# A fused RWKV-7, attention and MLP layer: the second tile of tokens is transposed as it comes, and its norm applied behind the products

## The chip, the cores and the metric

The kernel is one program on one core of a Trainium2 chip. The time is the device time of one execution in microseconds (us). The core has a matrix engine (TensorE, PE in the profile; its weight loads are listed apart as PEld), three engines for elementwise work (VectorE or DVE, ScalarE or ACT, GpSimd or POOL) and a queue for DMAs (SyncE, SP). Each engine works through its own list of instructions in order; semaphores make one engine wait for another.

## The reference, cut to what matters

One decoder layer on 256 tokens of 1024 numbers. The input is normalised, and one wide projection feeds three users:

```python
h = rms_norm(x, norm1_g[l])          # x * rsqrt(mean(x*x) + 1e-6) * g, per token
proj = h @ w_in[l]                   # (256, 1024) @ (1024, 5408)
z_rwkv, z_moba, gate_pre = ...       # columns 0:1824, 1824:3360, 3360:5408
z_rwkv = z_rwkv + rwkv_mu[l] * (shift_right(z_rwkv) - z_rwkv)   # mix with the token before
y_a = rwkv7_time_mix(z_rwkv, ...)    # r, k, v (512 columns each), xw, xa, xg (low rank)
q = partial_rope(rms_norm(q, q_norm_g[l]), positions)           # and k alike
y_b = moba_attention(q, k, v)        # here: causal attention over 256 tokens
x = x + (sigmoid(gate_a) * (y_a @ w_branch_a) + sigmoid(gate_b) * (y_b @ w_branch_b)) @ w_out
x = x + conv_ffn(rms_norm(x, norm2_g[l]), ...)
```

A norm's number per token (1 / root of the mean square) is a factor of a whole row of `h`, so it may as well be applied to the row of a product `x*g @ w`.

## The kernel before

**Precision.** Every wide product is made of three passes: a float32 operand is split into a rounded high part and the rest, and high*high, high*low and low*high are summed. For each 512 KB block of weights (`raw`, 128x1024), ScalarE makes the high part (`whi`, line L263) and VectorE the low part (`wlo`, L273); there are 122 such blocks, 4 raw, 4 high and 3 low buffers. A raw buffer is loaded again when its low part is done. The activations' parts are `hh` and `hl` (one tile `hx`).

**Staging.** `first_steps` is written out by hand for all engines: the load of x (two tiles of 128 tokens, four DMAs of 256 KB), the squares and root of each tile (`ss`, `rs`), the scaled rows `xn`, eight transposes per tile into PSUM (`xt`, L427), the split into `hh` and `hl` (L434, L436, L439) and the first products with the blocks 0 and 1 (`first`, L466, the columns of xw, xa, xg). Matrix-engine dummies (`keep_warm`, L388) run ahead of and between the transposes. Then two threads run, interleaved by hand-given costs: `bulk` makes the projections in order (k, r, q, v, attention's v, a gate, attention's k, seven gates, the branches), and `chain` the RWKV recurrence. TensorE's order comes from that interleaving, and the orders of VectorE, ScalarE and GpSimd from a scheduler that places instructions by estimated times.

**What the steps below touch.** `proj2` makes 256 columns of a projection over all tokens in one PSUM tile `p` (two groups of 128 columns by 256 tokens) from two blocks. `shift(dst, p, i)` turns it into a mixed `z`: one ScalarE instruction (L364) that reads `p`, then one of VectorE (L365). `finish_qk` norms attention's q and k per head; `rotate` applies the rotary angles on VectorE (L1061 to L1064). `group_norm` norms the recurrence's output, one chunk of 64 tokens at a time; GpSimd makes the power -1/2 (L931) and VectorE multiplies (L932).

Of the kernel before, what the change touches and what calls it, by code (L numbers as in the profile page):

```python
# [19 lines left out]
D = 1024  # L20
# [16 lines left out]
def body(tc, x, positions, norm1_g, w_in, rwkv_mu, w_decay_up, decay_bias, w_aaa_up,  # L37
# [5 lines left out]
    with ctx:  # L43
# [22 lines left out]
        def b2(name, shape, dt=F32):  # L66
            return sb.tile(shape, dt, name=name, tag="b2", bufs=9)
# [71 lines left out]
        G1, MU, DB, AB, KK_, KA, RK, LG, LB = 0, 8, 23, 27, 31, 35, 39, 43, 47  # L139
        omm = cst.tile([128, 15], F32, name="omm")  # L140
        omka = cst.tile([128, 4], F32, name="omka")

        pts = []

# [14 lines left out]
        def col(i):  # L159
            return par[:, i:i + 1]  # L160

        wdu = cst.tile([128, CW], F32, name="wdu")
# [197 lines left out]

        mixed = []

        def shift(dst, p, i):
            act.activation(dst, p, AF.Copy, scale=omm[:, i:i + 1])  # L364
            mixed.append(dve.scalar_tensor_tensor(dst[:, 1:S], p[:, 0:S - 1], col(MU + i), dst[:, 1:S],  # L365
                                                  op0=OP.mult, op1=OP.add).ins)
# [3 lines left out]
        def first_steps():  # L370
# [15 lines left out]
            def keep_warm(n):  # L386
                for _ in range(n):
                    pe.matmul(p, ones[:, 0:128], ones, start=True, stop=True)  # L388
# [10 lines left out]
            rs = sb.tile([128, 2], F32, name="rs1")  # L399
            bk = [b("xt") for b in (chp, chp, chp, atp, atp, acc, acc)]  # L400

            def at(k):
                return bk[min(k, 6)][:, 0 if k < 7 else 256:256 if k < 7 else 512]

            for t in range(2):
                xn = [b2("xn1", [128, 512]) for _ in range(2)]
                for hf in range(2):
                    act.activation(xn[hf], x_sb[t][:, hf * 512:hf * 512 + 512], AF.Square,
                                   accum_out=ss[:, t, hf:hf + 1])
                    if hf == 0:  # L410
                        dve.tensor_scalar(ss[:, t, 0:1], ss[:, t, 0:1], 1.0 / D, NORM_EPS,
                                          op0=OP.mult, op1=OP.add)
                act.activation(rs[:, t:t + 1], ss[:, t, 1:2], AF.Sqrt, scale=1.0 / D, bias=ss[:, t, 0:1])
                dve.reciprocal(rs[:, t:t + 1], rs[:, t:t + 1])
                for hf in range(2):
                    src = x_sb[t][:, hf * 512:hf * 512 + 512]
                    if t and hf:
                        act.activation(xn[hf], src, AF.Copy, scale=rs[:, t:t + 1])
                    else:
                        dve.tensor_scalar(xn[hf], src, rs[:, t:t + 1], None, op0=OP.mult)  # L420
                if t == 0:
                    pt = bk[5][:, 256:264]
                    pe.transpose(pt, p0, ident[:8, :8])
                    keep_warm(2)
                    dve.tensor_copy(par[:, 0:8], pt)
                for k in (0, 1, 2, 3, 4, 6, 7, 5):
                    pe.transpose(at(k)[:, t * 128:t * 128 + 128], xn[k // 4][:, k % 4 * 128:k % 4 * 128 + 128],  # L427
                                 ident)
                if t == 0:
                    keep_warm(3)  # L430

            def high(k):
                if k in (1, 3):
# [9 lines left out]
            for b in range(2):  # L443
# [4 lines left out]
            raw, hi, lo = w[0]  # L448
            for cs in (slice(0, 512), slice(512, 1024)):
                pool.tensor_copy(hi[:, cs], raw[:, cs])  # L450
            for k in range(8):
                high(k)
            for cs in (slice(0, 512), slice(512, 1024)):
                pool.tensor_tensor(lo[:, cs], raw[:, cs], hi[:, cs].bitcast(F32), op=OP.subtract)
            act.copy(w[1][1], w[1][0])
            for k in range(8):
                low(k)
            raw, hi, lo = w[1]
            for cs in (slice(0, 512), slice(512, 1024)):
                pool.tensor_tensor(lo[:, cs], raw[:, cs], hi[:, cs].bitcast(F32), op=OP.subtract)  # L460

            def first(b, lo_, xx, ks=(0, 1, 2, 3)):
                wv = w[b][lo_ + 1].rearrange("p (k c) -> p k c", k=4)
# [4 lines left out]
                                  skip_group_check=True)  # L468

            pts.append(atp("pt"))  # L470
            first(0, 0, hh)
            first(0, 1, hh, (0, 1))
            first(0, 0, hl)
            first(0, 1, hh, (2, 3))
            params_turned()
            late_params()
            split_hi()
# [2 lines left out]
            split_lo()  # L480

            first(1, 0, hh)
            first(1, 1, hh, (0, 1))
            first(1, 0, hl)
            first(1, 1, hh, (2, 3))
            late_consts()
            tl = chp("tl")[:, 0:S]
            for n, xx in enumerate((hh, hl)):
# [9 lines left out]
            dve.tensor_copy(tls, tl)  # L498
            shift(xg, p[:, 256:512], 13)
            split_lo()  # L500
            split_hi()
# [7 lines left out]
        def proj2():  # L509
            p = acc()  # L510
            yield from wst(p, 2, hh, hl)
            return p

        def now(gen):
# [48 lines left out]
        def chain():  # L563
# [352 lines left out]
            def group_norm():  # L916

                for c in range(4):
                    yield from need(c, ny)
                    y = ny[c]  # L920
                    cs = slice(64 * c, 64 * c + 64)
                    st = sb.tile([128, 3, 4], F32, name="st", tag="st", bufs=2)
                    dve.tensor_reduce(st[:, 0], y, axis=AX.X, op=OP.add)
                    dve.tensor_scalar(st[:, 0], st[:, 0], -1.0 / N, None, op0=OP.mult)
                    yc, sq2 = t1("yc", (128, 4, 64)), t1("sq2", (128, 4, 64))
                    dve.tensor_tensor(yc, y, st[:, 0][:, :, None].to_broadcast([128, 4, 64]), op=OP.add)
                    act.activation(sq2, yc, AF.Square)
                    yield 0, 0.8
                    dve.tensor_reduce(st[:, 1], sq2, axis=AX.X, op=OP.add)
                    dve.tensor_scalar(st[:, 1], st[:, 1], 1.0 / N, GN_EPS, op0=OP.mult, op1=OP.add)  # L930
                    pool.tensor_tensor(st[:, 2], st[:, 1], eps1[:, 1:2].to_broadcast([128, 4]), op=OP.pow)  # L931
# [83 lines left out]
        inv_last = []  # L1015
        later, x0_last = [], []

        def finish_qk(p, i, t):

            d = qkv[i][:, t]  # L1020
            if i == 2:
                act.copy(d.rearrange("p h n -> p (h n)"), p)
                return
            s2 = b2("s2", [128, 512])
            act.activation(s2, p, AF.Square)
            r2 = sb.tile([128, 8], F32, name="r2", tag="r2", bufs=2)
            with tc.high_priority():
                dve.tensor_reduce(r2, s2.rearrange("p (h n) -> p h n", h=8), axis=AX.X, op=OP.add)
                if i:
                    dve.tensor_scalar(r2, r2, 1.0 / N, NORM_EPS, op0=OP.mult, op1=OP.add)  # L1030
                    pool.tensor_tensor(r2, r2, eps1[:, 1:2].to_broadcast([128, 8]), op=OP.pow)
                else:
                    act.activation(r2, r2, AF.Sqrt, scale=1.0 / N, bias=eps1[:, 0:1])
                    dve.reciprocal(r2, r2)
                if i:
                    act.copy(d.rearrange("p h n -> p (h n)"), p)
                else:
                    dve.tensor_tensor(d, p.rearrange("p (h n) -> p h n", h=8),
                                      r2[:, :, None].to_broadcast([128, 8, 64]), op=OP.mult)
                    rotate(i, t)  # L1040
            if i:
                later.append((t, r2))
# [379 lines left out]
```

## Time and profile before

| | |
|---|---|
| time, median of 3 runs (lowest, highest) | 407.1 us (406.77, 407.61) |
| the profiled execution | 407.71 us, its span 405.6 us |
| TensorE busy | 399.1 us, 98% of the span |
| VectorE, ScalarE, GpSimd busy | 317.8, 234.3 and 44.5 us |
| DMA | 70.35 MB, 173 GB/s over the span |
| chain that ended last | PE 92%, DVE 3%, ACT 1%, DMA 1% |

The span runs from the first to the last instruction; the profiled execution's time is 2.1 us more than its span. A row of the timeline has the start, the duration (of several instructions, where it ends in x2 and more: from the first start to the last end), the engine, the line, the operation, output <- input with their shapes, and in brackets the idle time before it and what ended that. A row's duration is a little longer than the pace at which its engine goes on: rows of VectorE that follow one another overlap by some 0.08 us.

### The profile page before, as it was taken

How to read it: one execution, taken by the hardware profiler on the slowest of the kernel's cores; microseconds unless marked ns; L12 is line 12 of the kernel's file. 1: busy time of each engine (PE TensorE's matmuls, PEld its weight loads, DVE VectorE, ACT ScalarE, POOL GpSimd, SP SyncE). 2: the span in 40 equal slices, each digit the busy share in tenths (PEclk: the TensorE clock that was granted, in tenths of full speed). 3: DMA queues.
4: the chain of work that ended last, by engine and by line, in shares of the span. 5: the costliest groups of instructions: out<-in, count | busy, mean ns of one | idle time of the engine just before them, and what ended most of it. 6: DMA issues, size and time to landing. Idle time of an engine off the chain costs nothing.

```text
span 405.6 us, 8306 instructions
## 1 busy us (share of the span) xinstructions
PE 399.1 (98%) x3286; PEld 348.0 (86%) x3286; DVE 317.8 (78%) x539; ACT 234.3 (58%) x395; POOL 44.5 (11%) x72
## 2 busy tenths in 40 slices
PE   6999999999999999999999999999999999999996
PEld 3899899888899898999888888888888888888885
DVE  3888999869576797687965897967869778697694
ACT  5999665365464975453554764555545455365450
POOL 7810510122320010000000000000000000000000
PEclk9999999999999999999999999999999999999999
DMA  8983556755845244446665657566655656656612
GB/s 238 315 255 101 160 155 161 205 137 136 229 114 152 55 156 125 159 136 198 178 197 155 200 161 214 160 210 200 207 185 176 207 178 188 205 174 197 199 56 105
DMA packets 60193, 70.35 MB, mean 173 GB/s; under 512 B 7608, under 2 KB 50506, under 8 KB 60154
## 3 DMA queue, kind: packets, MB, share of 16 engines
q1 hardware_dynamic: 59222, 69.40, 57.2%
q0 software_dynamic: 880, 0.41, 0.6%
q8 instruction: 26, 0.43, 0.4%
q14 instruction: 13, 0.11, 0.1%
q10 hardware_dynamic: 52, 0.01, 0.0%
HBM read 68.37 MB, written 1.44 MB: 172 GB/s over the span
## 4 chain that ended last, share of the span: by engine, by line
PE 92%; DVE 3%; DMA 1%; ACT 1%; issue 1%; POOL 0%; SPq 0%; ACTq 0%
PE acc L1303 20%; PE acc L1308 10%; PE acc L301 8%; PE acc L306 7%; PE acc L303 7%; PE acc L322 5%; PE acc L326 5%; PE acc L323 5%; PE f L1325 4%; PE f L1323 4%; PE f L1327 4%; PE idle L466 1%; DMA x<-in_x_dram 1%; PE pgr L687 1%; DVE sc L1119 1%
## 5 line engine op out<-in xcount | busy, mean ns | idle before, releaser
L263 ACT CAST whi<-raw 128x1024 fp32r<-128x1024 f32 x122 | 127.8, 1052 | 110.8 <-PE acc L1303 42.5
L273 DVE TENSOR_TENSOR wlo<-raw,whi 128x1024 fp32r<-128x1024 f32 x122 | 149.5, 1228 | 38.6 <-PE acc L1308 14.0
L1303 PE MATMUL acc<-hx,whi 128*128 128x512 f32 x352 | 89.5, 396 | 0.0
L1303 PEld LDWEIGHTS acc<-hx,whi 128*128 128x128 f32 x352 | 63.5, 188 | 12.4
L301 PE MATMUL acc<-hx,whi 128*128 128x256 f32 x224 | 56.9, 289 | 0.0
L303 PE MATMUL acc<-hx,whi 128*128 128x256 f32 x224 | 54.6, 279 | 0.0
L1308 PEld LDWEIGHTS acc<-hx,wlo 128*128 128x128 f32 x352 | 46.8, 188 | 4.0
L1308 PE MATMUL acc<-hx,wlo 128*128 128x256 f32 x352 | 47.4, 277 | 0.0
L301 PEld LDWEIGHTS acc<-hx,whi 128*128 128x128 f32 x224 | 42.2, 189 | 2.5 <-issue 1.4
L303 PEld LDWEIGHTS acc<-hx,whi 128*128 128x128 f32 x224 | 42.2, 189 | 0.1
L306 PE MATMUL acc<-hx,wlo 128*128 128x256 f32 x224 | 35.0, 278 | 0.0
L1325 PE MATMUL f<-whi,hb 128*128 128x512 f32 x80 | 31.2, 390 | 0.0
L1323 PE MATMUL f<-whi,hb 128*128 128x512 f32 x80 | 31.2, 390 | 0.0
L1327 PE MATMUL f<-wlo,hb 128*128 128x512 f32 x80 | 31.2, 390 | 0.0
L306 PEld LDWEIGHTS acc<-hx,wlo 128*128 128x128 f32 x224 | 30.0, 189 | 0.0
L1313 DVE TENSOR_REDUCE an<-acc 128x256 f32<-128x512 f32 x22 | 14.2, 685 | 9.4 <-PE acc L1308 9.3
L322 PE MATMUL acc<-whi,hx 128*128 128x512 f32 x48 | 19.5, 406 | 0.0
L323 PE MATMUL acc<-whi,hx 128*128 128x512 f32 x48 | 18.8, 392 | 0.0
L1327 PEld LDWEIGHTS f<-wlo,hb 128*128 128x128 f32 x80 | 15.0, 188 | 3.2
L1323 PEld LDWEIGHTS f<-whi,hb 128*128 128x128 f32 x80 | 15.0, 188 | 2.8
L1325 PEld LDWEIGHTS f<-whi,hb 128*128 128x128 f32 x80 | 15.0, 188 | 2.7
L326 PE MATMUL acc<-wlo,hx 128*128 128x512 f32 x48 | 14.9, 393 | 0.0
(336 smaller groups left out, 627.8 us busy)
## 6 DMA issues: line engine op xcount, KB each, us to landing
raw<-in_w_ffn_up_dram SPq DMA_DIRECT2D x44, 512.0 KB, 4.2
raw<-in_w_in_dram SPq DMA_DIRECT2D x41, 512.0 KB, 3.8
raw<-in_w_ffn_down_dram SPq DMA_DIRECT2D x22, 512.0 KB, 3.9
raw<-in_w_out_dram SPq DMA_DIRECT2D x8, 512.0 KB, 4.0
x<-in_x_dram SPq DMA_DIRECT2D x8, 256.0 KB, 3.7
raw<-in_w_branch_b_dram SPq DMA_DIRECT2D x4, 512.0 KB, 4.1
raw<-in_w_branch_a_dram SPq DMA_DIRECT2D x4, 512.0 KB, 4.3
out_dram<-o SPq DMA_DIRECT2D x3, 256.0 KB
```

The lines of the kernel that those rows point to most:

```text
L263: act.copy(hi[:, :k * c], raw[:, :k * c])
L273: eng.tensor_tensor(lo[:, :n], raw[:, :n], hi[:, :n].bitcast(F32), op=OP.subtract)
L301: pe.matmul(om, wh[:, k, ms], xh[:, k0 + k], start=k0 + k + m == 0, stop=False, skip_group_check=True)
L303: pe.matmul(om, wh[:, k, ms], xl[:, k0 + k], start=False, stop=False, skip_group_check=True)
L306: pe.matmul(om, wl[:, k, ms], xh[:, k0 + k], start=False, stop=k0 + k == nk - 1 and m == n - 1, skip_group_check=True)
L322: pe.matmul(ps_[t], xh[:, K, ts], wh[:, k], start=K == 0, stop=False)
L323: pe.matmul(ps_[t], xl[:, K, ts], wh[:, k], start=False, stop=False)
L1303: pe.matmul(ps_[m], wh[:, k, m * 128:m * 128 + 128], hx[:, k0 + k].rearrange("p a s -> p (a s)"), start=k0 + k == 0, stop=False, skip_grou ...
L1308: pe.matmul(ps_[m][:, 0:S], wl[:, k, m * 128:m * 128 + 128], hh[:, k0 + k], start=False, stop=k0 + k == 7, skip_group_check=True)
L1323: pe.matmul(fin[f], hb[:, 0, i, ts], wh[:, 0, cs], start=st, stop=False, skip_group_check=f == 3)
L1325: pe.matmul(fin[f], hb[:, 1, i, ts], wh[:, 0, cs], start=False, stop=False, skip_group_check=f == 3)
L1327: pe.matmul(fin[f], hb[:, 0, i, ts], wl[:, 0, cs], start=False, stop=False, skip_group_check=f == 3)
```

## The change

The root of the second tile is no longer on the way to its transposes: the rows of tile 2 (`x_sb[1]`) are transposed raw, and their numbers (`r1`) applied to every product's token columns 128:256. For products with tokens along the columns, `r1` is spread over a tile `rbc` (128x128, by a copy, a transpose and a copy), and a new VectorE instruction `second(p)` multiplies both groups of `p` in place ahead of `shift` or of a gate's tanh; that is 15 more VectorE instructions on PSUM (one in `first_steps`, six for k, r and v, eight for the gates), and one for the thin product `tl`. For products with tokens along the partitions (attention's q, k, v), `r1` is a scale of an instruction that is there already.

In `first_steps`, tile 2's first half is transposed ahead of tile 1, three dummies go, block 0's high part is cast in quarters, one half of each low part of blocks 0 and 1 goes from GpSimd to VectorE, and each `first(0, 0, hh)` is followed by its `hl`. In `group_norm`, GpSimd multiplies three of four chunks. In the diff, the call of `second` is in `proj2` and that of `num` (an activation with `scale=r1` for the second tile) in `finish_qk`.

```diff
-            for t in range(2):
-                xn = [b2("xn1", [128, 512]) for _ in range(2)]
...
+            square(0, 0)
+            square(0, 1)
+            root(0)
+            square(1, 0)
+            for hf in range(2):
+                dve.tensor_scalar(xn[hf], x_sb[0][:, hf * 512:hf * 512 + 512], rs[:, 0:1], None, op0=OP.mult)
...
+            keep_warm(2)
+            dve.tensor_copy(par[:, 0:8], pt)
+            for k in range(4):
+                turn(1, k)
+            for k in (0, 1, 2, 3, 4, 6, 7, 5):
+                turn(0, k)
+            for k in (4, 6, 7, 5):
+                turn(1, k)
...
+            for cs in quarters:
+                pool.tensor_copy(w[0][1][:, cs], w[0][0][:, cs])
+            for k in (0, 1, 2, 3, 4, 6, 7, 5):
                 high(k)
             act.copy(w[1][1], w[1][0])
+            lower(0, halves_[0], pool)
+            for k in range(4):
+                low(k)
+            lower(0, halves_[1], dve)
+            for k in (4, 6, 7, 5):
+                low(k)
+            square(1, 1)
+            lower(1, halves_[0], pool)
+            lower(1, halves_[1], dve)
+            root(1)
+            rx = t1("rx1", (128, 128))
+            dve.tensor_copy(rx, r1.to_broadcast([128, 128]))
...
+            pe.transpose(pts[0][:, 128:256], rx, ident)
+            dve.tensor_copy(rbc, pts[0][:, 128:256])
...
+        def second(p):
+            v = p.rearrange("p (m c) -> p m c", m=2)[:, :, 128:256]
+            dve.tensor_tensor(v, v, rbc[:, None, :].to_broadcast([128, 2, 128]), op=OP.mult)
...
             yield from wst(p, 2, hh, hl)
+            second(p)
...
-                    dve.tensor_tensor(yc, yc, st[:, 2][:, :, None].to_broadcast([128, 4, 64]), op=OP.mult)
+                    (dve if c == 3 else pool).tensor_tensor(
+                        yc, yc, st[:, 2][:, :, None].to_broadcast([128, 4, 64]), op=OP.mult)
...
-            act.activation(s2, p, AF.Square)
+            num(s2, p, AF.Square, t)
```

TensorE's list stays as it was apart from `first_steps` and one group of four transposes that moves by three products. The other lists are laid anew by the scheduler. Three places of VectorE's list matter below.

The start of VectorE's list, ahead of the first sums: `ones` feeds the dummies, `rowf` and `spread_90` are masks for the recurrence, made from the identity `ident` that GpSimd writes. Before:

```order
L381 MEMSET ones 128x512
L382 MEMSET eps_84 128x1
L383 MEMSET eps_84 128x1
L132 TENSOR_REDUCE rowf<-ident 128x1
L134 TENSOR_SCALAR spread_90<-rowf 128x64
L135 TENSOR_SCALAR spread_90<-rowf 128x64
```

The same place now:

```order
L132 TENSOR_REDUCE rowf<-ident 128x1
L134 TENSOR_SCALAR spread_90<-rowf 128x64
L135 TENSOR_SCALAR spread_90<-rowf 128x64
L389 MEMSET ones 128x512
L390 MEMSET eps_84 128x1
L391 MEMSET eps_84 128x1
```

The masks have moved ahead of `ones`, which now stands behind a wait for `ident`.

The parts of `hx` and the first low parts on VectorE, up to the first mix (`par`, `omm`, `omka`: parameters turned; `idle` is the PSUM tile of the first products). Before:

```order
L439 SCALAR_TENSOR_TENSOR hx<-xt,par,hx 128x256 x8
L150 COPY par<-pt 128x43
L151 TENSOR_SCALAR omm<-par 128x15
L152 TENSOR_SCALAR omka<-par 128x4
L273 TENSOR_TENSOR wlo<-raw,whi 128x1024
L365 SCALAR_TENSOR_TENSOR xwa<-idle,par,xwa 128x255
```

And now:

```order
L453 SCALAR_TENSOR_TENSOR hx<-xt,par,hx 128x256 x4
L467 TENSOR_TENSOR wlo<-raw,whi 128x512
L453 SCALAR_TENSOR_TENSOR hx<-xt,par,hx 128x256 x4
L418 TENSOR_SCALAR ss_160<-ss_160 128x1
L467 TENSOR_TENSOR wlo<-raw,whi 128x512
L423 RECIPROCAL rs<-rs 128x1
L485 COPY rx_232<-rs 128x128
L153 COPY par<-pt 128x43
L154 TENSOR_SCALAR omm<-par 128x15
L155 TENSOR_SCALAR omka<-par 128x4
L276 TENSOR_TENSOR wlo<-raw,whi 128x1024
L513 COPY rbc<-pt 128x128
```

Half of each early low part, the second tile's sum `ss_160`, its root and its spreading now stand between the low parts of `hx` and the mix, and `second` and the mix follow the last row.

The end of attention's q on VectorE, while the recurrence's inputs are made (`KB`, `AR`: its keys and queries; `r_811`, `r_823` and now `r_818`, `r_830`: q's norms of tile 1 and 2; `ro`: rotary products). Before:

```order
L273 TENSOR_TENSOR wlo<-raw,whi 128x1024
L1028 TENSOR_REDUCE r_811<-s_809 128x8
L656 TENSOR_TENSOR AR<-zr,sg 128x16x64
L273 TENSOR_TENSOR wlo<-raw,whi 128x1024
L1034 RECIPROCAL r_811<-r_811 128x8
L794 SCALAR_TENSOR_TENSOR zr<-zr,par,kp 128x256
L1028 TENSOR_REDUCE r_823<-s_821 128x8
L1038 TENSOR_TENSOR qkv<-acc,r_811 128x512
L1034 RECIPROCAL r_823<-r_823 128x8
L1061 TENSOR_TENSOR ro<-qkv,rot 128x128
L1038 TENSOR_TENSOR qkv<-acc,r_823 128x512
L1061 TENSOR_TENSOR ro<-qkv,rot 128x128 x3
```

And now, from the same low part on:

```order
L276 TENSOR_TENSOR wlo<-raw,whi 128x1024
L1066 TENSOR_REDUCE r_830<-s_828 128x8
L687 TENSOR_TENSOR AR<-zr,sg 128x16x64
L1072 RECIPROCAL r_818<-r_818 128x8
L1072 RECIPROCAL r_830<-r_830 128x8
L1076 SCALAR_TENSOR_TENSOR qkv<-acc,r_818 128x512
L1076 SCALAR_TENSOR_TENSOR qkv<-acc,rs,r_830 128x512
L1099 TENSOR_TENSOR ro<-qkv,rot 128x128 x4
L1101 TENSOR_TENSOR qkv<-ro 128x8x8 x2
L1102 TENSOR_TENSOR qkv<-ro 128x8x8 x2
L276 TENSOR_TENSOR wlo<-raw,whi 128x1024 x2
```

The low part that stood ahead of q's scaling and rotation (the second `wlo` of the rows of before) now stands behind all of it, next to the one that follows.

More of the change, by code (lines that the diff above doesn't have):

```diff
@@ L141, in body @@
         omka = cst.tile([128, 4], F32, name="omka")
+        rs = cst.tile([128, 2], F32, name="rs")
+        rbc = cst.tile([128, 128], F32, name="rbc")
+        r1 = rs[:, 1:2]
         pts = []
@@ L160, in col @@
             return par[:, i:i + 1]
-        wdu = cst.tile([128, CW], F32, name="wdu")
+        wdu = b2("wdu", [128, CW])
         wgu = b2("wgu", [128, CW])
@@ L403, in at @@
                 return bk[min(k, 6)][:, 0 if k < 7 else 256:256 if k < 7 else 512]
-            for t in range(2):
-                xn = [b2("xn1", [128, 512]) for _ in range(2)]
[L407 to L412, printed above, removed]
+            xn = [b2("xn1", [128, 512]) for _ in range(3)]
@@ L413, in first_steps, with square, root @@
+            def square(t, hf):
+                act.activation(xn[2], x_sb[t][:, hf * 512:hf * 512 + 512], AF.Square,
+                               accum_out=ss[:, t, hf:hf + 1])
+                if hf == t:
+                    dve.tensor_scalar(ss[:, t, 0:1], ss[:, t, 0:1], 1.0 / D, NORM_EPS,
+                                      op0=OP.mult, op1=OP.add)
+            def root(t):
                 act.activation(rs[:, t:t + 1], ss[:, t, 1:2], AF.Sqrt, scale=1.0 / D, bias=ss[:, t, 0:1])
                 dve.reciprocal(rs[:, t:t + 1], rs[:, t:t + 1])
[L415 to L430, printed above, removed]
+            def turn(t, k):
+                src = x_sb[t][:, k * 128:k * 128 + 128] if t else xn[k // 4][:, k % 4 * 128:k % 4 * 128 + 128]
+                pe.transpose(at(k)[:, t * 128:t * 128 + 128], src, ident)
@@ new lines, in first_steps @@
+            square(0, 0)
[4 more added lines that the diff above has]
+                dve.tensor_scalar(xn[hf], x_sb[0][:, hf * 512:hf * 512 + 512], rs[:, 0:1], None, op0=OP.mult)
+            pt = bk[5][:, 256:264]
+            pe.transpose(pt, p0, ident[:8, :8])
+            keep_warm(2)
[4 more added lines that the diff above has]
+                turn(0, k)
@@ L447, in first_steps, with lower @@
                 w.append((raw, hi, lo))
[L448 to L451, printed above, removed]
+            quarters = [slice(256 * i, 256 * i + 256) for i in range(4)]
+            halves_ = (slice(0, 512), slice(512, 1024))
+            def lower(b, cs, eng):
+                raw, hi, lo = w[b]
+                eng.tensor_tensor(lo[:, cs], raw[:, cs], hi[:, cs].bitcast(F32), op=OP.subtract)
+            for cs in quarters:
+                pool.tensor_copy(w[0][1][:, cs], w[0][0][:, cs])
+            for k in (0, 1, 2, 3, 4, 6, 7, 5):
                 high(k)
-            for cs in (slice(0, 512), slice(512, 1024)):
-                pool.tensor_tensor(lo[:, cs], raw[:, cs], hi[:, cs].bitcast(F32), op=OP.subtract)
             act.copy(w[1][1], w[1][0])
-            for k in range(8):
+            lower(0, halves_[0], pool)
+            for k in range(4):
                 low(k)
-            raw, hi, lo = w[1]
-            for cs in (slice(0, 512), slice(512, 1024)):
-                pool.tensor_tensor(lo[:, cs], raw[:, cs], hi[:, cs].bitcast(F32), op=OP.subtract)
+            lower(0, halves_[1], dve)
[7 more added lines that the diff above has]
+            dve.tensor_copy(rx, r1.to_broadcast([128, 128]))
             def first(b, lo_, xx, ks=(0, 1, 2, 3)):
@@ L470, in first_steps @@
             pts.append(atp("pt"))
-            first(0, 0, hh)
+            for k in range(4):
+                first(0, 0, hh, (k,))
+                first(0, 0, hl, (k,))
+            first(0, 1, hh, (2, 3))
             first(0, 1, hh, (0, 1))
-            first(0, 0, hl)
-            first(0, 1, hh, (2, 3))
             params_turned()
@@ L482, in first_steps @@
             first(1, 0, hh)
-            first(1, 1, hh, (0, 1))
             first(1, 0, hl)
             first(1, 1, hh, (2, 3))
+            first(1, 1, hh, (0, 1))
+            pe.transpose(pts[0][:, 128:256], rx, ident)
+            dve.tensor_copy(rbc, pts[0][:, 128:256])
             late_consts()
@@ L511, in proj2 @@
             yield from wst(p, 2, hh, hl)
+            second(p)
             return p
@@ L1016, in body, with num @@
         later, x0_last = [], []
+        def num(dst, p, f, t):
+            if t:
+                act.activation(dst, p, f, scale=r1)
+            else:
+                act.activation(dst, p, f)
         def finish_qk(p, i, t):
@@ L1035, in finish_qk @@
                 if i:
[L1036 removed]
+                    num(d.rearrange("p h n -> p (h n)"), p, AF.Copy, t)
                 else:
[L1038 to L1039 removed]
+                    dve.scalar_tensor_tensor(d, p.rearrange("p (h n) -> p h n", h=8), r1 if t else 1.0,
+                                             r2[:, :, None].to_broadcast([128, 8, 64]), op0=OP.mult, op1=OP.mult)
                     rotate(i, t)
```

6 lines of the change are left out of this document (3 added, 3 removed).

## The prediction

> **What bounds the kernel now.** I read the page's head and its slices first, then the busy time by stretch, and then the timeline of the first 20 us and of 35 to 65 us, engine by engine.
>
> ```profile
> span 405.6 us, 8306 instructions
> PE 399.1 (98%) x3286; PEld 348.0 (86%) x3286; DVE 317.8 (78%) x539; ACT 234.3 (58%) x395; POOL 44.5 (11%) x72
> PE   6999999999999999999999999999999999999996
> DVE  3888999869576797687965897967869778697694
> ```
>
> TensorE is busy from the second slice to the last but one. So a change is worth what it moves the first product forward, less every hole that it tears into TensorE's row later. VectorE has an average of 78%, but slices 5 to 7 (41 to 71 us) read 9, 9, 9 or close to it. By stretch:
>
> ```profile
> 18.05:37.50 19.45, 19.45 (x165) 18.61 (x162) 15.54 (x37) 18.92 (x34) 3.90 (x8) 1.00 0.62 190
> 37.50:60.40 22.90, 22.90 (x154) 19.75 (x153) 22.84 (x30) 16.67 (x25) 7.58 (x15) 1.00 0.59 167
> 60.40:65.30 4.90, 4.90 (x59) 4.71 (x58) 4.90 (x16) 3.24 (x9) 0.00 (x0) 1.00 0.46 125
> ```
>
> The columns behind the length are PE, PEld, DVE, ACT and POOL. From 18 to 37.5 us ScalarE works 18.92 of 19.45 us, and from 37.5 to 65.3 us VectorE 27.74 of 27.80. TensorE has no hole there, but two other engines are as full as it is: what they get on top is not free.
>
> **The first product.**
>
> ```profile
> 0.91 0.48 DVE L381 MEMSET ones<- 128x512 bf16 x1 [0.91 <-PEq L1410]
> 1.46 3.58 PE L388 MATMUL idle<-ones 128*128 128x512 bf16 x8 [1.46 <-DVE eps L383]
> 2.13 0.19 DVE L135 TENSOR_SCALAR spread<-rowf 128x64 f32<-128x64 f32 x1
> 7.37 0.63 ACT L408 ACTIVATE xn<-x 128x512 f32<-128x512 f32 x1 [1.13 <-DMA x<-in_x_dram]
> 8.09 1.52 POOL L450 CAST whi<-raw 128x512 fp32r<-128x512 f32 x2 [1.29 <-DMA raw<-in_w_in_dram]
> 9.18 0.86 PEld L427 LDWEIGHTS xt<-ident,xn 128*128 128x128 f32 x8 [1.63 <-DVE xn L420]
> 10.14 0.99 PEld L466 LDWEIGHTS idle<-hx,whi 128*128 128x128 f32 x8
> ```
>
> Before, tile 2 lands at 7.37, is squared, rooted and scaled, and its transposes start only at 9.18; products follow at 10.14. Now `ones` stands behind the masks: VectorE is through with them at 2.13+0.19 = 2.32, so the dummies start 1.3 us later, at about 2.8, and end, with the two behind them, at about 6.9. Sixteen transposes at 0.86/8 = 0.107 us take 1.7 us; the last four need what landed at 7.37, which is past by then. They end at 8.6. The first quarter of the high part is there at 8.09 + 1.52/4 = 8.5. So the first product comes at 8.6 in place of 10.14: 1.5 us earlier. The transpose of `rx` costs TensorE 0.1 of it. This much the change can win.
>
> **VectorE, GpSimd and ScalarE behind it.**
>
> ```profile
> 9.57 2.54 POOL L454 TENSOR_TENSOR wlo<-raw,whi 128x512 fp32r<-128x512 f32 x2
> 10.46 3.22 DVE L439 SCALAR_TENSOR_TENSOR hx<-xt,par,hx 128x256 fp32r<-128x256 f32 x8
> 11.71 1.08 ACT L455 CAST whi<-raw 128x1024 fp32r<-128x1024 f32 x1
> 12.65 1.09 ACT L263 CAST whi<-raw 128x1024 fp32r<-128x1024 f32 x1
> 12.87 2.54 POOL L460 TENSOR_TENSOR wlo<-raw,whi 128x512 fp32r<-128x512 f32 x2 [0.76 <-ACT whi L455]
> 14.17 2.32 DVE L273 TENSOR_TENSOR wlo<-raw,whi 128x1024 fp32r<-128x1024 f32 x1
> 16.34 0.47 ACT L364 ACTIVATE xwa<-idle,omm 128x256 f32<-128x256 f32 x1
> 18.05 1.98 ACT L263 CAST whi<-raw 128x1024 fp32r<-128x1024 f32 x2
> ```
>
> Tile 2's root is not gone, it has moved: its sum on VectorE now stands behind all eight low parts of `hx`, the root on ScalarE waits for it, and ScalarE's cast of block 2 (12.65 before) stands behind the root. VectorE's low parts start at about 8.5 (two high parts of 0.4 each after the first transposes), four take 1.6 to 10.1, then comes half a low part of block 0. Alone it takes half of 1.2. But GpSimd makes the other half at that time (9.6 to 10.9), and the row at 14.17 shows 2.32 us for what takes 1.2 elsewhere: it lay beside GpSimd's low parts until 15.41. So 0.6 alone, up to 1.4 beside; I take the upper, since this is the same pair of operations. Four more low parts, sum and root: 13.5 (12.7 if alone). The cast that was at 12.65 is 0.85 late (0.05 if alone). From it to the end of the next two casts ScalarE needs 3.5 (12.65 to 16.2), so `xwa` is mixed at 17.0 in place of 16.34, and the casts of the row at 18.05, which started 1.7 later, start at 18.7 (17.9 if alone). TensorE is ahead by then and does not mind; ScalarE is behind.
>
> [...]
>
> **ScalarE to 37 us.** From the casts at 18.05 ScalarE is full, so its work keeps its length.
>
> ```profile
> 35.49 0.47 ACT L364 ACTIVATE zk<-acc,omm 128x256 f32<-128x256 f32 x1
> 37.52 1.22 DVE L624 TENSOR_TENSOR kp<-kp,zk 128x1024 f32<-128x1024 f32 x1
> ```
>
> The last of k's four mixes started 17.44 behind 18.05. Now a cast (0.95) stands ahead of it, and the 0.5 of idle time can go (it waited there for TensorE, which is ahead now): 17.9, or 17.7 with the shorter bubbles of three multiplications in a row. With 0.47 for itself and 0.4 to 0.5 for VectorE's half, `kp` starts 18.6 to 18.8 behind the casts; I take the lower, since no wait for TensorE is left there: 37.3 (18.7 + 18.6), against 37.52 before.
>
> **VectorE to 65 us.** Here the change bites. `second` is not in the trace. The nearest rows are a product of PSUM and SBUF of the same 256 columns, and a full 512 of such work (61.33 below):
>
> ```profile
> 96.87 1.09 DVE L832 TENSOR_TENSOR zr<-pg,zv 128x256 f32<-128x256 f32 x3
> 59.13 1.22 DVE L273 TENSOR_TENSOR wlo<-raw,whi 128x1024 fp32r<-128x1024 f32 x1
> 60.73 0.68 DVE L1028 TENSOR_REDUCE r<-s 128x8 f32<-128x512 f32 x1
> 61.33 0.69 DVE L1038 TENSOR_TENSOR qkv<-acc,r 128x512 f32<-128x512 f32 x1
> 61.92 0.20 DVE L1034 RECIPROCAL r<-r 128x8 f32<-128x8 f32 x1
> 62.12 0.29 DVE L1061 TENSOR_TENSOR ro<-qkv,rot 128x128 f32<-128x128 f32 x1
> 62.32 0.68 DVE L1038 TENSOR_TENSOR qkv<-acc,r 128x512 f32<-128x512 f32 x1
> 62.92 0.68 DVE L1061 TENSOR_TENSOR ro<-qkv,rot 128x128 f32<-128x128 f32 x3
> 63.53 0.35 DVE L1063 TENSOR_TENSOR qkv<-ro 128x64 f32<-128x64 f32 x2
> 63.80 0.35 DVE L1064 TENSOR_TENSOR qkv<-ro 128x64 f32<-128x64 f32 x2
> 64.07 1.21 DVE L273 TENSOR_TENSOR wlo<-raw,whi 128x1024 fp32r<-128x1024 f32 x1
> 63.59 0.64 PE L306 MATMUL acc<-hx,wlo 128*128 128x256 f32 x4
> ```
>
> So `second` takes 0.36 to 0.7; I take 0.4, its own size. The low part that VectorE made at 59.13 to 60.35 is the one that TensorE's products at 63.59 read (I counted blocks from the start: two groups of low products for each low part). It had 3.2 us in hand. From the start of `kp` to its end VectorE worked 60.27 - 37.52 = 22.75 us without a pause. Now all from 60.27 to 64.07 (3.8) but one instruction of 0.35 stands ahead of it, and two `second` of r (0.8): 4.25 are added (4.15 to 4.85 with the bounds of `second`). Waits for ScalarE's root of the recurrence's norm, which now is asked for earlier, I put at 0.1 (-0.2 to 0.3). That makes 22.75 + 4.25 + 0.1 = 27.1, and the low part ends at 37.3 + 27.1 + 0.1 = 64.5. TensorE, up to 1.5 us ahead, reaches it at about 62.5 and waits 2 us: it goes on 0.9 behind its old time of 63.59. What was won at the start is spent, and 0.9 more.
>
> The next low part stands right behind (65.6 for products that were at 66.4), and after it VectorE has room again, so TensorE goes on without holes, all of it 0.9 late.
>
> **What else is added.** Eight `second` for gates lie between 92 and 175 us, and where VectorE is fullest there, low parts are far ahead:
>
> ```profile
> 144.96 1.22 DVE L273 TENSOR_TENSOR wlo<-raw,whi 128x1024 fp32r<-128x1024 f32 x1
> 145.13 1.92 POOL L931 TENSOR_TENSOR st<-st,eps 128x4 f32<-128x4 f32 x1 [30.64 <-DVE st L930]
> 152.55 0.64 PE L306 MATMUL acc<-hx,wlo 128*128 128x256 f32 x4
> ```
>
> This one waited 6.4 us for TensorE's products; two `second` of 0.4 there are covered, and what queues behind `second` while it waits for the end of a gate's products is such a low part and nothing else. If that cover were gone, each would cost 0.4. GpSimd's three multiplications take 0.42 each off VectorE and cost GpSimd about 0.65 (half of 1.27, the pace of L454), behind a power that took 1.92 us beside VectorE's low part: they may hold VectorE up as long as they spare it. I put that at 0, between -0.4 and +0.5. Attention's q, k and v keep their instructions and get a scale: 0.
>
> **The sum**, against the profiled execution: span 405.6 + 0.9 = 406.5, execution 407.7 + 0.9 = 408.6. The median of the runs, 407.1, lies 0.6 below the profiled one, so I predict 408.0. With all costs at their low ends (casts at 17.9, `kp` 18.6 behind, then 26.7) it is -0.3, at the high ends (18.8, 18.8, 27.9) +2.0: this case alone runs from 406.8 to 409.1.
>
> **The rivals.**
> - *The early start reaches the end.* If low part and products met without a wait, 1.5 us less the transpose and some 0.3 of holes in the first products would remain: -1.1, 406.0. It takes a low part at 62.5, so `kp` at 35.3. For it: VectorE would need less than the rows show, or ScalarE have less to do. Against it: the full rows of 18 to 65 us. It decides from a low part ready before 63.6. Chance 0.15.
> - *The middle costs more.* GpSimd's multiplications and VectorE's low parts hold one another up between 136 and 160 us, where VectorE is full and TensorE waits for its state updates; each of three such meetings can cost up to a low part's 1.2 us on VectorE, of which I let a third reach TensorE: +0.4 each on top, 409.2. The row at 145.13 speaks for it, the 6.4 us in hand against it. Chance 0.12.
> - *Nothing to measure*: the wait at 63.6 eats what the start wins and no more, because the half low parts do not collide or the waits for the root vanish: 407.1, between -0.8 and +0.1. Chance 0.13.
> [...]
>
> **How the numbers follow.** 0.2% of 407.1 is 0.8 us, about what a measurement of this kernel can tell from no change. The main case has 0.60; of its range (-0.3 to +2.0, with +0.9 the likeliest) somewhat more than half lies above +0.8, so 0.34 is slower and 0.26 the same. With the rivals: slower 0.34 + 0.12 = 0.46, same 0.26 + 0.13 = 0.39, faster 0.15. The range that holds the time 8 times in 10 reaches into the early-start case and the dear middle: 406.2 to 409.2.
>
> **What would show it.** Right: the first weights' product at 8.5 to 9 us; a low part of VectorE of 1.2 us or more for 512 columns beside GpSimd's; ScalarE's casts that were at 18.05 at 18.2 to 18.7; and one hole of 1 to 2.5 us in TensorE's row at 62 to 65 us that waits for `wlo` behind the rotation, with no other hole above 0.5 us. Wrong: no hole there (then the early start wins and it is faster), or holes between 136 and 160 us (then it is the middle). A `second` of more than 0.7 us would make it slower than my range.

## The result: 410.9 us, 1% slower than before

The changed kernel takes 410.9 us (median of six executions, 409.78 to 415.14) where the kernel before took 406.98 in the same set; the ratio is 1.010 with a 95% interval of 1.006 to 1.014. That is 3.9 us more, and above the predicted range. The six differ more than usual: three with a mean matrix clock of 0.999 or 1.000 took 409.8 to 410.4, two with 0.996 took 411.5 and 411.6, and the one that was profiled, with 0.992, took 415.14 at a span of 413.4.

The head of its page, with TensorE's and VectorE's slices and the clock's:

```profile
span 413.4 us, 8322 instructions
PE 402.0 (97%) x3284; PEld 349.9 (85%) x3284; DVE 322.0 (78%) x555; ACT 234.5 (57%) x394; POOL 42.1 (10%) x75
PE   7999998999799999999999999999999999999996
DVE  3888998949384798677976898869779688697794
PEclk9999999999799999999999999999999999999999
```

Between its first and last slice, TensorE's row now has two under 9: the seventh (62 to 72 us) and the eleventh (103 to 114 us). In the second of them the granted clock falls too. The three stretches that were shown of before, in the same columns:

```profile
18.05:37.50 19.45, 19.45 (x169) 18.55 (x166) 16.09 (x40) 18.92 (x34) 1.38 (x3) 1.00 0.57 176
37.50:60.40 22.90, 22.66 (x152) 19.34 (x151) 22.78 (x30) 17.04 (x28) 6.80 (x15) 1.00 0.57 159
60.40:65.30 4.90, 3.30 (x44) 2.91 (x43) 4.90 (x15) 3.07 (x8) 0.00 (x0) 1.00 0.36 105
```

ScalarE (18.92) and VectorE (22.78 and 4.90) are as full as before; TensorE lost 1.84 us. **The first hole**, from VectorE's and TensorE's timelines:

```profile
38.06 1.22 DVE L655 TENSOR_TENSOR kp<-kp,zk 128x1024 f32<-128x1024 f32 x1
63.51 0.35 DVE L1102 TENSOR_TENSOR qkv<-ro 128x64 f32<-128x64 f32 x2
63.78 2.35 DVE L276 TENSOR_TENSOR wlo<-raw,whi 128x1024 fp32r<-128x1024 f32 x2
65.05 0.74 PE L309 MATMUL acc<-hx,wlo 128*128 128x256 f32 x4 [1.60 <-DVE wlo L276]
```

This is the hole that the prediction placed here: the low part behind q's rotation is done at 65.0, TensorE waits 1.60 us for it and goes on 1.46 behind the 63.59 of before.

**The second hole** was not predicted. It lies in the recurrence, on the way from the pairwise products to the inverse of its 16x16 blocks. VectorE masks the products (`G`), the blocks go by DMA to a buffer and back (`Tb`), VectorE inverts them (from the copy `Xb<-Tb` on), and they go by DMA once more into the tile `X0` (named X in the rows), which TensorE's product `pp` reads. First the rows of before, then of after:

```profile
77.38 2.48 DVE L691 TENSOR_TENSOR G<-pgr,gmask 128x512 f32<-128x512 f32 x4
87.91 0.18 DVE L728 COPY Xb<-Tb 128x12 f32<-128x12 f32 x1 [1.86 <-DMA Tb<-d]
99.73 2.25 POOL L771 DMA_DIRECT2D X<-d x4 [3.10 <-DMA d<-Xb]
102.99 0.73 PE L851 MATMUL pp<-X,G 32*32 32x16 f32 x64
```

```profile
80.07 2.48 DVE L722 TENSOR_TENSOR G<-pgr,gmask 128x512 f32<-128x512 f32 x4
91.75 0.18 DVE L759 COPY Xb<-Tb 128x12 f32<-128x12 f32 x1 [3.63 <-DMA Tb<-d]
103.44 2.25 POOL L802 DMA_DIRECT2D X<-d x4 [3.08 <-DMA d<-Xb]
107.26 0.20 PE L882 MATMUL pp<-X,G 32*32 32x16 f32 x2 [2.14 <-DMA X<-d]
108.20 1.04 PE L882 MATMUL pp<-X,G 32*32 32x16 f32 x62 [0.74 <-DMA X<-d]
```

Before, the blocks come just in time: no wait at `pp`. After, `G` is 2.7 us later (1.6 of it the first hole, 1.1 its place in VectorE's list), the trip of the blocks takes 11.7 us from the start of the last four `G` to the inverse and not 10.5, and the DMAs that fill `X0` and the tile of the next step take 3.3 to 3.4 us each (median, from issue to landing) and not 1.9 to 2.1. TensorE, itself 2.1 us late, stands still for 2.9 us. So the later `G` makes some 0.6 us of this hole, and the two trips of small DMAs, 1.15 and 1.3 us longer, make the rest. And then its clock halves (PE busy, then the granted clock; TensorE alone, in steps of one us):

```profile
106.00:107.00 1.00, 0.00 (x0) 1.00 0.70 64
107.00:108.00 1.00, 0.20 (x2) 0.74 0.50 58
108.00:109.00 1.00, 0.80 (x60) 0.50 0.81 87
113.00:114.00 1.00, 1.00 (x3) 0.50 0.43 129
114.00:115.00 1.00, 1.00 (x63) 0.85 0.05 18
```

The ledger, by the time at which the same instruction starts in the two traces: the thin product `tl` +0.05 us (16.24 and 16.29), first pairwise product +1.57 (68.39, 69.96), `pp` +4.3, the first product behind the second group of `pp` +7.87 (107.27, 115.14), end of span +7.8. Behind 115 us nothing more is lost.

### The profile page after: what moved, and what is told of

The parts are those of the page before. It is cut to its first block, busy times and chain, and to the rows that moved or that the text cites. A ratio compares the mean times of both kernels' runs of the same rounds, so it can differ in the third digit from the quotient of the medians.

```text
span 413.4 us, 8322 instructions
## 1 busy us (share of the span) xinstructions
PE 402.0 (97%) x3284; PEld 349.9 (85%) x3284; DVE 322.0 (78%) x555; ACT 234.5 (57%) x394; POOL 42.1 (10%) x75
## 4 chain that ended last, share of the span: by engine, by line
PE 79%; DVE 10%; ACT 4%; DMA 4%; issue 2%; POOL 1%; SPq 0%; POOLq 0%; DVEq 0%; ACTq 0%
PE acc L1341 20%; PE acc L1346 10%; PE acc L304 5%; PE acc L309 5%; PE acc L306 5%; PE f L1363 4%; PE f L1361 4%; PE f L1365 4%; PE acc L325 3%; DVE wlo L276 3%; PE acc L326 3%; PE acc L329 2%; PE idle L491 1%; ACT whi L266 1%; PE idle L396 1%
## 5 line engine op out<-in xcount | busy, mean ns | idle before, releaser
L325 PE MATMUL acc<-whi,hx 128*128 128x512 f32 x48 | 20.4, 426 | 0.0
L326 PE MATMUL acc<-whi,hx 128*128 128x512 f32 x48 | 19.7, 411 | 0.0
```

The source lines that it names most:

```text
L325: pe.matmul(ps_[t], xh[:, K, ts], wh[:, k], start=K == 0, stop=False)
L326: pe.matmul(ps_[t], xl[:, K, ts], wh[:, k], start=False, stop=False)
```

## The experiments

One trace is taken of each kernel, and the other executions give only times and mean clocks. The theory after the result (A in the expectations): two holes, the first from the low part's place behind the rotation, the second from the blocks' late arrival, and behind it a slow clock in some executions. The rivals: B, the 16 added instructions of VectorE cost their time wherever they stand; C, the late dummies; D and E on the half low parts and GpSimd's norms. Each time stands beside the kernel before, run in the same set.

### e1: the low part ahead of the rotation again

```diff
-            with tc.high_priority():
+            with (tc.high_priority() if i else ExitStack()):
                 dve.tensor_reduce(r2, s2...)     # finish_qk; i = 0 is attention's q
```

> The changed kernel with one difference: the norm and rotation of attention's q lose their priority over the weights' low parts, so that two low parts stand ahead of the rotation again in VectorE's list. Theory A (two holes: TensorE waits 1.6 us at 63.4 for a low part, and at 104.9 for the inverse's blocks that come by DMA, the second followed by a slow matrix clock in some executions): the first hole goes, the pairwise products are back at 68.4 to 68.8, and the second hole is left as it is, since the blocks and TensorE come earlier together: 408.5 to 409.5. Theory B (VectorE has too much work in all, and a hole that is closed opens at another place): TensorE waits as much elsewhere before 110 us, 410 to 411, no faster than the changed kernel.

Measured: 406.65 us against 407.02, ratio 1.0003 (0.9989 to 1.0017). All of the loss is gone, with the added instructions still there. The first hole is gone, and of the second little is left. The two waits of TensorE's timeline between 60 and 110 us that are longer than 0.2 us:

```profile
78.98 0.66 PE L819 MATMUL pv<-ident,zv 128*128 128x128 f32 x4 [0.97 <-DVE G L722]
102.86 0.70 PE L882 MATMUL pp<-X,G 32*32 32x16 f32 x62 [0.60 <-DMA X<-d]
```

It was better than expected: the pairwise products came at 66.24, not at 68.4 to 68.8, so TensorE was 2.15 us ahead of before there (1.1 of it at `tl` already), and 1.0 of it is left at the end. Theory B falls as the cause of the 3.9 us; what the instructions do cost is the matter of e5, e6 and e12.

### e2 and e3: the product with the blocks later

```diff
-            yield 0, 5.5
+            yield 0, 8.0
             pp = two_banks("pp", 16)
```

> The changed kernel with one difference: the first product with the inverse's blocks stands 12 products (2.7 us) later in TensorE's list. Theory A: the wait of 2.9 us at 105 falls to under 0.5 us, the granted clock of 100 to 120 us is 1.00, the wait of 1.6 us at 63.4 stays, and the time is 408.5 to 409.3 in all executions, with less spread. Theory B: 410 to 411; so would be the case that the clock falls for another reason than the hole (clock under 1.00 in that stretch without a hole).

> Both differences at once. Theory A: neither hole, span within 0.6 us of the kernel before, 407.0 to 407.8. Theory B: at least one other hole of 1 us or more, 409 or more.

Measured: 412.54 (ratio 1.0135, 1.012 to 1.015) and 412.82 (1.0126, 1.0108 to 1.0144): worse, against theory A's expectation. The wait at `pp` went in both, but the recurrence ended later and branch a waited for it. The waits in TensorE's timeline of e3 there:

```profile
183.70 0.41 PE L972 MATMUL pc<-ident,yc 128*128 128x128 f32 x2 [0.91 <-DVE yc L963]
187.95 0.62 PE L304 MATMUL acc<-yah,whi 128*128 128x256 f32 x3 [1.02 <-ACT yah L977]
189.18 0.38 PE L306 MATMUL acc<-yal,whi 128*128 128x256 f32 x1 [0.61 <-DVE yal L978]
```

So from `pp` on the recurrence has no time to spare: a wait there can't be hidden behind other products, it comes back at the branch. In e2 the first hole was as in the changed kernel (1.59 us), though 0.88 us earlier, and this time it was followed by the slow clock (the columns as above):

```profile
64.17 0.78 PE L309 MATMUL acc<-hx,wlo 128*128 128x256 f32 x4 [1.59 <-DVE wlo L276]
```

```profile
65.00:66.00 1.00, 1.00 (x6) 0.50 0.80 96
```

### e4: the second hole made without the change

```diff
-            yield 0, 5.5        # in the kernel before
+            yield 0, 3.0
```

> The kernel before, with the first product with the inverse's blocks 12 products (2.7 us) sooner in TensorE's list, so that the hole of the changed kernel is made without the change. Theory A: a hole of 2 to 3 us at 100 us that ends on the DMA of the blocks, in some executions followed by 5 us or so at a clock of 0.5 to 0.6: 409 to 412, with mean clocks below 1.000 in the longer ones. If the hole alone doesn't throttle the clock: 409.5 at clock 1.000 in all. If TensorE's time there is given back later (the recurrence ends sooner): 407.

Measured: 411.12 us (409.72 to 413.38), ratio 1.0107 (1.0082 to 1.0131). The kernel before, with a hole at `pp` of 2.5 us, is as slow as the changed kernel, and it spreads in the same way: 409.72 and 410.84 at clock 1.000, 410.62 and 411.39 at 0.996, 412.78 and 413.38 at 0.992. The two waits in the timeline, and one step of the clock behind them:

```profile
100.94 0.20 PE L851 MATMUL pp<-X,G 32*32 32x16 f32 x2 [1.71 <-DMA X<-d]
101.92 0.70 PE L851 MATMUL pp<-X,G 32*32 32x16 f32 x62 [0.78 <-DMA X<-d]
```

```profile
103.00:104.00 1.00, 1.00 (x4) 0.50 0.71 84
```

### e5 and e6: the multiplications taken out, and put in alone

```diff
             yield from wst(p, 2, hh, hl)
-            second(p)                        # e5, from the changed kernel
+            second(p)                        # e6, into the kernel before, rbc = 1.0
```

> The changed kernel without the 14 multiplications of the projections (the one in the start stays), so that tile 2 of r, k, v and the gates is left without its norm. In VectorE's list the low part then stands ahead of the rotation. Theory A (the place of that low part is what costs, not the multiplications' time): no hole at 63, a time like that of e1_qfinish_low, 406.0 to 406.9. Theory B (14 times 0.34 us of VectorE are paid): at least 1.5 us below e1_qfinish_low, 405 or less.

> The kernel before with 14 such multiplications by a tile of ones, and nothing else of the change. TensorE's list stays, and the low part stays ahead of the rotation. Theory A: the multiplications alone are covered, no hole above 0.5 us at 60 to 66, 407.0 to 407.8. Theory B: 14 times 0.34 is 4.8 us of VectorE's time in its full stretch, of which 1.5 us or more reach TensorE: 408.5 to 411.

Measured: e5 406.68 against 407.55, ratio 0.9975 (0.9962 to 0.9988); e6 409.19 against 407.55, ratio 1.0049 (1.0026 to 1.0072). e5's time is the one that A expected, but e1 was run beside a kernel before of 407.02: set against its own kernel before, e5 is 0.5 us (by the medians) to 1.1 us (by the ratios) below e1, between A and B. e6 is as B expected, 1.6 us by the medians and 2.0 by the ratio. So the multiplications do cost something by themselves, though not 3.9 us. e6 also moves `wdu` to a shared buffer, as the change does, and its `ones` stand behind the masks; its thin product `tl` is no later for that (15.82). One multiplication takes what was assumed; e6's groups have (busy us, mean ns behind the bar):

```profile
L369 DVE TENSOR_TENSOR acc<-acc,rbc 128x256 f32<-128x256 f32 x14 | 5.9, 423 | 3.3 <-PE acc L306 3.2
```

Their price does not come at 60 to 65 us, where VectorE is fullest: e6 has no hole there. It comes between the recurrence's first state and branch a, where TensorE's timeline has one wait of more than 0.2 us:

```profile
148.07 0.76 PE L990 MATMUL pS<-VU,KBt 128*64 128x64 f32 x14 [0.83 <-DVE VU L984]
```

TensorE needs 53.9 us for that stretch (131.88 to 185.80) where before needed 52.8.

### e7 and e12: GpSimd's norms, alone and with the multiplications

The edit is the change's own in `group_norm`.

> The kernel before with only the recurrence's three norms scaled by GpSimd. Theory A: nothing, 406.7 to 407.4. The rival of the prediction (GpSimd and VectorE hold one another up in the middle): 407.4 to 408.3, with holes of TensorE between 130 and 160 us.

> e6_before_second (14 multiplications by ones, 409.2) with the recurrence's norms scaled by GpSimd as well. Theory E (the eight multiplications for the gates were paid between 131 and 174 us, where VectorE is full, and GpSimd's three make room for them): TensorE needs 53.9 us from the recurrence's first state to branch a there in e6 and 52.4 to 52.8 here, 407.6 to 408.2. If the two don't depend on one another: 409.2 less 0.3, 408.9.

Measured: e7 407.23 against 407.55, ratio 0.9986 (0.9975 to 0.9998), so a little gain and no harm; e12 407.73 against 407.40, ratio 1.0012 (1.0000 to 1.0023), with 52.7 us for the stretch that took 53.9 in e6. GpSimd's three products make room for the gates' eight: the two edits hang together. Between e7 and e12 the multiplications cost 0.7 us by the medians, 1.1 by the ratios.

### e8: the last four `G` first as well

The edit is e1's, and in VectorE's list the eight `G` (`glast`) ahead of low part 21 and of the products `bp`:

```diff
+                nlo[0] += 1
+                with (tc.issue_after(glast[-1]) if nlo[0] == 21 and len(glast) == 8 else ExitStack()):
+                    eng.tensor_tensor(lo[:, :n], raw[:, :n], hi[:, :n].bitcast(F32), op=OP.subtract)
...
+                with tc.issue_after(glast[-1]):
+                    dve.scalar_tensor_tensor(bp[:, ct], zr[:, ct], col(RK + ct), kp[:, ct],
+                                             op0=OP.mult, op1=OP.mult)
```

> e1_qfinish_low with the second four products G (pairwise products times their mask) ahead of one low part and of the four products of r and k in VectorE's list. Theory A with its continuation (what the early start wins is lost again at the inverse's blocks, because their input G waits in VectorE's list): G ends 1.5 to 2 us earlier, the waits of 1.0 us for G and 0.6 us for the blocks go, 405.0 to 405.8. Rival: the recurrence's later steps or the branches take it back: 406.4 to 406.9, with a new hole behind 110 us.

Measured: 405.52 us (405.16 to 405.71) against 407.55, ratio 0.9943 (0.9927 to 0.9959). This beats the kernel before by 2.0 us and, by the two ratios, the changed kernel by some 6. No group of TensorE's products has more than 0.2 us of waits behind the start.

### e9 and e10: `ones` ahead of the masks again

```diff
-            with tc.issue_after(last_exp[-1]):
+            with tc.issue_after(par_in[0]):      # behind the copy of norm1_g
                 masks()
```

> The changed kernel with the three masks behind the scaling of tile 1 in VectorE's list, so that `ones` and the dummies come as early as before. Theory C (the late dummies leave the matrix clock cold for the transposes, which is why the first product came at 9.64 and not at 8.6): dummies at 1.5, the four transposes of tile 2's first half take 0.6 us and not 1.06, first product at 8.2 to 8.7. Theory A adds: TensorE then meets the low part behind the rotation all the earlier, that hole grows by as much as the start wins, and the time stays within 0.8 us of the changed kernel's 410.3. Rival (the start's gain reaches the end): 409 or less.

> e8_masks_first with `ones` ahead of the three masks again. Theory C: first product at 8.2 to 8.7, each later stage as early, 0.5 to 1.0 us under e8_masks_first: 404.5 to 405.1. If VectorE or ScalarE's full stretch takes it back: a new hole before 110 us and the time of e8_masks_first, 405.3 to 405.7.

Measured: e9 409.08 against 407.40, ratio 1.0054 (1.0032 to 1.0076), below the changed kernel's 1.010, but the two intervals overlap; e10 405.61 in the same set, ratio 0.9954 (0.9940 to 0.9968), no better than e8. TensorE's start in the changed kernel, then in e9, then in e13 (below), whose `ones` stand behind the masks as in the changed kernel:

```profile
6.65 1.03 PE L396 MATMUL idle<-ones 128*128 128x512 bf16 x2
7.47 1.06 PE L427 MATMUL xt<-ident,x 128*128 128x128 f32 x4
9.64 2.39 PE L491 MATMUL idle<-hx,whi 128*128 128x256 f32 x16
16.29 1.93 PE L519 MATMUL tl<-hx,wtr 128*32 128x256 f32 x32
```

```profile
5.05 0.60 PE L397 MATMUL idle<-ones 128*128 128x512 bf16 x2
5.49 0.60 PE L428 MATMUL xt<-ident,x 128*128 128x128 f32 x4
7.91 0.50 PE L492 MATMUL idle<-hx,whi 128*128 128x256 f32 x2
64.21 0.73 PE L310 MATMUL acc<-hx,wlo 128*128 128x256 f32 x4 [1.59 <-DVE wlo L277]
```

```profile
6.55 0.60 PE L399 MATMUL idle<-ones 128*128 128x512 bf16 x2
6.99 0.60 PE L430 MATMUL xt<-ident,x 128*128 128x128 f32 x4
```

Theory C's rows came, but they don't show its cause. The last two dummies and the first four transposes are slow (1.03 and 1.06 us) in the changed kernel, e3 and e5, quick (0.60 or 0.61) in e1, e2 and e13, and between the two in e8, and in all seven the dummies start at 2.9 us. In e11 they start at 1.46, as in e9, and the pair is slow (1.03 and 1.06). So it differs from trace to trace, with `ones` in either place. The granted clock reads 1.00 in all of these stretches: no trace shows the cold clock of theory C there, nor what else slowed them. Nor does `ones` first show a gain at the thin product `tl`: it starts at 15.41 in e9, and at 15.14 to 15.41 in e1, e2 and e13.

A's addition fell, as did its time (409.5 or more): the hole at 64 us did not grow by what the start won, it kept its 1.59 us and came 0.84 us earlier. It did so too in e2 (64.17) and e13 (64.06), where the start was quick without this edit. The stages behind the start move with it. Why e10 is not better than e8 is open: it is 1.1 us ahead up to 170 us, loses 0.3 to branch a and 0.4 behind it, and no group of its products there has more than 0.2 us of waits. The intervals of the two overlap.

### e11: the half low parts back on GpSimd

The edit gives both `lower(..., dve)` back to GpSimd, in e10, and lets the products of each of the two low parts stand in one group again.

> e10_masks_and_ones_first with the two half low parts of the start back on GpSimd. Theory D (with these on VectorE, TensorE's first 48 products are paced by VectorE's low parts of hx, 6.65 us where 6.1 were needed before): 6.1 to 6.2 from the first product to the thin product `tl`, `xwa` mixed 0.4 earlier, 0.3 to 0.6 us under e10. Rival: GpSimd's low parts come later than the products want them, 6.6 or more, no gain.

Measured: 405.67, ratio 0.9963 (0.9949 to 0.9977): no gain. From the first product to `tl` 7.05 us pass (8.37 to 15.42), in e10 7.19 (7.73 to 14.92). Theory D falls.

### e13 and e14: the last four `G` first, without e1

> The changed kernel with only the second difference of e8_masks_first: the second four G ahead of one low part and of the four products of r and k; the low part stays behind the rotation. Theory A (two separate causes): the hole of 1.6 us at 63 stays and shifts all behind it; G ends 3.7 us behind the start of its products in place of 4.9, the blocks come in time, no wait at pp, clock 1.000 in most executions: 1.5 to 2.2 us above before, 408.5 to 409.3. If the second hole were only a consequence of the first: still 1 us or more of wait at pp, 410 or more.

> The kernel before with the second four G ahead of one low part and of the products of r and k. TensorE has no wait at pp there, so the blocks coming sooner is worth nothing: 406.7 to 407.4, ratio 0.998 to 1.001. If e8_masks_first owes its gain to this place alone and not to the change: 405.5, ratio 0.995.

Measured: e13 408.19 against 407.40, ratio 1.0037 (1.0012 to 1.0061); its executions at clock 0.999 or more took 407.7 to 409.0, three others with 0.996 and 0.992 took 412.2 to 414.2. By the times of the first group it is what A expected, 1.5 us above before by the ratio: the first hole kept and the second closed. But the profiled execution (0.992) doesn't show it: there the first hole of 1.60 us was followed by the slow clock, the trip from `G` to the inverse took 9.9 us, `pp` waited 3.2 us all the same (2.8 of it put down by the profile to a low part that ended just then, which `pp` does not read), and a second stretch of the slow clock followed. e14 went against the expectation: 409.44, ratio 1.0061 (1.0038 to 1.0084), with 1.3 us of waits at `pp` (half of it again beside the end of a low part), because the trip took 9.9 us there as well and not 8.05. So `G` first is no gain in itself. Over the traces the trip, from the end of `G` to the inverse, takes 6.7 to 6.9 us (e8, e10, e11), 7.3 to 8.4 (before, e1 to e7, e9, e12), 9.2 (after) and 9.9 (e13, e14). There is one trace of each kernel, so how much of this differs from execution to execution isn't shown. Half of these DMAs stand in SyncE's queue among weight loads, whose places move with VectorE's list; which load costs what was not tried.

## Why the prediction was wrong, point by point

- **First product at 8.6, 1.5 us won.** In the trace of the changed kernel it came at 9.64, where the last two dummies and the first transposes were slow. In e1, e2 and e13, which have the same start, it came at 8.32 to 8.76, as predicted. The sum leaves a slow start out, but it moves what follows: `tl` lies at 16.29 to 16.46 in the three traces in which they are slow (the changed kernel, e3, e5), and at 15.14 to 15.41 in those three. In before's own trace it lies at 16.24, in the variants of before at 15.72 (e7) to 16.56 (e12). And part of the win is gone by `tl`: the changed kernel needs 6.65 us for the first products where before needed 6.07. Why isn't shown; with the half low parts taken off VectorE (e11) it was no less.
- **The half low part, 1.4 us beside GpSimd's in place of 0.6.** No run shows the 1.4. In the changed kernel the half low part took 0.68 us; GpSimd was through 0.3 us before it began. In e1, beside GpSimd's for its first 0.31 us, it took 0.85. The casts came at 18.96 in this trace, not at 18.7, and at 17.80 to 18.08 in e1, e2 and e13. In the row at 14.17 of before, 1.08 of the 2.32 us lie behind the end of GpSimd's low parts (15.41); alone such a low part takes 1.22 us, so some 0.14 of it was done beside them.
- **`kp` at 37.3.** 38.06. From the casts to `kp` it took 19.1 us, in this trace as in e1, e2 and e13, and not the 18.6 that were taken: where no wait of ScalarE for TensorE was assumed, one of 0.27 us (at 20.27) stayed. In e2 `kp` came at 37.18, near the forecast, by luck: the casts 0.6 earlier than said, and the stretch 0.5 longer.
- **The low part at 64.5, TensorE waits 2 us, net +0.9.** The mechanism was right, and e1 shows it. From `kp` to the end of the low part it took 26.9 us, against 27.1 forecast. In e2 TensorE came at 62.58 and waited 1.59, close to the forecast (62.5 and 2), for a net of +0.58. In the trace of the changed kernel the net is +1.46, because its slow start left TensorE a lead of 0.14 us only. The hole is the same 1.6 in both, since VectorE's work moves with the start.
- **`second` 0.4 us.** 0.42. The six for k, r and v are covered as long as the low part is early (e6). That the eight for the gates are covered holds only with GpSimd's norms (e6 against e12), and then all but some 0.7 to 1.1 us of the fourteen's cost (e7 against e12).
- **"It goes on without holes, all of it 0.9 late".** This is the step that failed. It looked at VectorE's low parts alone. The other chain through VectorE's list, `G` to `X0`, takes 23.7 us from its second group of products (76.08) to the DMA that fills `X0` (99.73), and TensorE came to `pp` with almost nothing to spare: in e14 the same DMA comes 1.6 us later behind those products, and `pp` waits 1.3, so before had some 0.3 us in hand. The rows were in the trace of before. A delay that reaches `G` twice, through TensorE's products and through VectorE's list, had to open a hole there: `G` is 2.7 us late and TensorE 2.1, which makes one of 0.3 to 0.6 us. The rest of the 2.9 is the DMAs of this chain, 2.4 us slower in all, and why they were slower stays open. With the clock behind it this hole is the larger part of the loss: of the span's 7.8 us in the profiled execution some 6. Of the 3.9 us of the medians 2.4 are left once the first hole's 1.5 are taken off, but that is a subtraction, not a measurement. e4 shows that a hole at `pp` alone makes such a loss, and e13's times (408.19, near the predicted 408.0) fit a kernel with the first hole only.
- **The rivals.** Holes at 136 to 160 us: none in the changed kernel, but e6 shows that they were a matter of 1 us or so. The chances gave too little to "something else waits".

## What to carry to other kernels

When an engine's list is laid anew, list every chain that leaves that engine and comes back to the bottleneck, and write down for each how long its result had been there when it was read; those with nothing to spare set the price, however far they are from the edit. A hole in the matrix engine can cost twice its length when the slow clock follows it (2.9 us of waits and 3.4 us of lost clock in the changed kernel's trace). Before a change is judged, try the order apart from the work: here the multiplications cost some 0.5 to 1.1 us (e5 against e1, e7 against e12), and the order of the lists the 3.9 us that e1 won back. And one trace is one execution: the start of this kernel differed by 1 us between traces with the same start, as much as the change was meant to win.

## What the runs showed of the hardware

- The clock falls to 0.50, and for stretches of 3.4 us. Worked out from the rows in steps of one us: in e2 from 64.74 to 68.14 (3.40 us), in e4 from 102.68 to 106.10 (3.42), after the change from 107.48 to 114.30 (6.82, two of them), in e13 from 64.30 to 67.72 and from 108.68 to 112.10 (3.42 each). One stretch loses 1.7 us, 0.4% of an execution, so the mean clocks 0.996 and 0.992 fit one and two of them. What starts a stretch isn't shown: in e2 and in e13 one followed the first hole (1.59 and 1.60 us), and in the changed kernel and in e9 none followed the same hole at the same place (1.60 and 1.59).
- A chain of small DMAs through memory (`G` to the inverse) took between 6.7 and 9.9 us for the same work, one trace each. The pairs that differ in VectorE's order alone are e1 and e8 (7.3 and 6.7), the changed kernel and e13 (9.2 and 9.9), before and e14 (8.05 and 9.9).
- Beside GpSimd's low part for its first 0.31 us, VectorE's half low part took 0.85 us in e1 (9.87 to 10.72, GpSimd's until 10.18), and 0.68 alone: 0.17 more for an overlap of 0.31. In before's row at 14.17, 1.10 more (2.32 against 1.22) for an overlap of 1.24. In both, what it lost is 0.14 us less than the overlap.
